# Every second feed-forward weight chunk gets its lower half by an adding transfer instead of a VectorE subtraction

## The chip, the cores and the metric
The kernel runs on one core of a Trainium2 chip. The time is what the device takes for one launch, in microseconds. Before the change three runs took 1796.32 to 1797.32 us, median 1796.88 us. A separate execution was taken by the hardware profiler; durations and waits below come from that one.

## The reference
Two model blocks of two layers each, at 256 positions and width 1024, all in float32. The first block is a mixer of four branches with a context stream. The second block has, in each layer, a sequence mixer (a gated recurrent unit in layer 0, gated linear attention in layer 1) and a convolutional feed-forward part, which is what the change touches:

```python
def causal_dwconv(x, w, b):          # w (K,C), b (C)
    k_width = w.shape[0]
    s = x.shape[1]
    xp = jnp.pad(x, ((0, 0), (k_width - 1, 0), (0, 0)))
    y = b
    for k in range(k_width):
        y = y + xp[:, k:k + s] * w[k]
    return y

def conv_ffn(h, w_up, conv_w, conv_b, w_down):
    u = causal_dwconv(h @ w_up, conv_w, conv_b)
    g, val = jnp.split(u, 2, axis=-1)
    return (jax.nn.gelu(g) * val) @ w_down
# per layer:
#   h = rmsnorm_2(x, norm_g[i, 2]) * (1.0 + sc_f) + sh_f
#   y = conv_ffn(h, ffn_w_up[i], ffn_conv_w[i], ffn_conv_b[i], ffn_w_down[i])
#   x = x + gt_f * rmsnorm_2(y, norm_g[i, 3])
```

w_up is 1024 x 5632 (22 tiles of 128 gate columns and 22 of value columns), w_down 2816 x 1024.

## The kernel before
Activations lie transposed: features on the 128 partitions, the 256 positions along the free dimension. A float32 product is made of three matmuls of a reduced-precision type (float32r): each operand is split into an upper half (the value rounded to that type) and a lower half (the value minus the upper half), and `mm3` adds upper x upper, upper x lower and lower x upper; the lower half of the weight is read by the third of each three.

Weights stream in chunks of 128 x 1024 (512 KB), one for each tile of 128 output columns. `load` brings one: SyncE issues the transfer into a raw tile `wr` (pool `wp`, 3 buffers), ScalarE writes the upper half `wh`, VectorE writes the lower half `wl` as `wr - wh`. `wh` and `wl` have 4 buffers each (`NW = 4`), so four chunks are held: when TensorE has finished with a chunk, `drop` lets the next load begin. `tile_gemm` takes a chunk and does 8 x 3 matmuls of 128 x 256 with it.

`ffn` first does four tiles at once (`start4`), while the normalised input is made, and then loops over the other 20 pairs of gate and value tiles: for each pair two chunks, two accumulators (one from each of two PSUM pools, `pm` and `pa`), the convolution of width 3 (ScalarE takes the last tap and the bias out of PSUM, VectorE adds two taps), GELU on ScalarE, the product on VectorE, and the split of the result (`r`, upper half on ScalarE, lower on VectorE). In the first layer this loop also runs `gla_prepare`, which clears ten buffers of the next layer on ScalarE, one step for each pair. After the loop `project_out` multiplies by w_down, again chunk by chunk.

The order of instructions on each engine is fixed when the program is built: a scheduler places them by its own estimate of when things become ready. On an engine they run strictly in that order, so an instruction that waits holds up all behind it; the same holds for the transfers that SyncE or GpSimd issue. In the first block and the start of the second, SyncE's queue also carries the rows of the modulation matrices (`ad`, two buffers), which VectorE multiplies and sums (`matvec`, `junk`). GpSimd does almost nothing: eight loads of 512 KB (`wf`, line 287) before the second block, and four small operations at the end.

Of the kernel before, what the change touches and what calls it, by code (L numbers as in the profile page):

```python
# [9 lines left out]
F32 = mybir.dt.float32  # L10
# [4 lines left out]
ALU = mybir.AluOpType  # L15
# [70 lines left out]
class Sum:  # L86


    def __init__(self, k=None, *tiles):
        self.k, self.acc, self.last = k, None, None  # L90
        self.tiles = list(tiles)
# [13 lines left out]
class Core:  # L105
    NW = 4

    def __init__(self, nc, tc, ctx, A):
        self.nc, self.tc, self.A = nc, tc, A
        pool = lambda n, b, **k: ctx.enter_context(tc.tile_pool(name=n, bufs=b, **k))  # L110
        self.cst = pool("cst", 1)
        self.wp = pool("wp", 3)
        self.whl = pool("whl", self.NW)
        self.xp = pool("xp", 1)
        self.sml = pool("sml", 16)
        self.rowp = pool("rowp", 2)
        self.mm = pool("mm", 4, space=PSUM)
        self.aux = pool("aux", 4, space=PSUM)
        self.hiq, self.loq = deque(), deque()
        self.src, self.ready, self.held = deque(), deque(), 0  # L120
        self.credit = 0.0
        self.last = self.late = None
        self.wide, self.tiles = 0, 0
        self.uid = 0
        self.pumps, self.spare, self.ratio = -100, 0.0, 0
        self.rows, self.raws = deque(), deque()
        self.marks = deque(maxlen=10)
# [129 lines left out]
    def load(self, src):  # L257
        n = 1
        for d in src.shape[1:]:
            n *= d  # L260
        raw = self.wp.tile([P, 1024], F32, tag="wr", name=self.nm("wr"))
        dst = raw[:, :n]
        if len(src.shape) == 3:
            dst = dst.rearrange("p (a b) -> p a b", a=src.shape[1])
        with self.behind():
            self.lastload = self.nc.sync.dma_start(out=dst, in_=src).ins
        hi = self.whl.tile([P, 1024], F32R, tag="wh", name=self.nm("wh"))
        lo = self.whl.tile([P, 1024], F32R, tag="wl", name=self.nm("wl"))

        def high():  # L270
            self.act(hi[:, :n], raw[:, :n])

        def low():
            self.tt(lo[:, :n], raw[:, :n], hi[:, :n].bitcast(F32), ALU.subtract)
        if self.late is None:
            with self.behind():
                high()
                low()
        else:
            self.late.extend([high, low])  # L280
        return hi, lo
# [1291 lines left out]
    def ffn(self, i, xs, mk, nxt):  # L1573
        w = self.A["ffu"][i]
        for c in range(2, NFF):
            self.src.extend([w[c], w[NFF + c]])
        self.src.extend(self.out_chunks(self.A["ffd"][i], NFF))
        fw = lambda k, c: self.par("ffn_conv_w_2", i * 132 + k * 44 + c)
        acts = []

        def conv(ps, c):
            t = self.T1()
            self.act(t, ps, AF.Identity, scale=fw(2, c), bias=self.par("ffn_conv_b_2", i * 44 + c))
            self.stt(t[:, 1:], ps[:, :S - 1], fw(1, c), t[:, 1:], ALU.mult, ALU.add)
            self.stt(t[:, 2:], ps[:, :S - 2], fw(0, c), t[:, 2:], ALU.mult, ALU.add)
            return t

        def glu(c, pg, pv):
            g = conv(pg, c)
            self.act(g, g, AF.Gelu_apprx_tanh)  # L1590
            v = conv(pv, NFF + c)
            self.tt(g, g, v, ALU.mult)
            acts.append(self.split1(g))

        ps, hs = self.start4(mk, S)
        self.wide = 2
        self.hiq.append(self.squares(xs))
        glu(0, ps[0], ps[2])
        glu(1, ps[1], ps[3])
        prep = self.gla_prepare() if i == 0 else iter(())  # L1600
        for c in range(2, NFF):
            if c > 3:
                next(prep, None)
            pg = self.tile1(hs)
            glu(c, pg, self.tile1(hs))
        self.wide = 0
        return self.project_out(i, 1, xs, acts, NFF, nxt)

    def gla_prepare(self):
# [213 lines left out]
def build(nc, tc, A):  # L1823
    with ExitStack() as ctx:
        k = Core(nc, tc, ctx, A)
        with ExitStack() as c1:
            k.adp = c1.enter_context(tc.tile_pool(name="adp", bufs=2, reuse_waits="tile"))
            k.setup()
            k.t2 = c1.enter_context(tc.tile_pool(name="t2", bufs=58, reuse_waits="tile"))
            fin = k.first_block()  # L1830
        k.t1 = ctx.enter_context(tc.tile_pool(name="t1", bufs=74, reuse_waits="tile"))
        k.g4 = ctx.enter_context(tc.tile_pool(name="g4", bufs=12, reuse_waits="tile"))
        k.second_block(*fin)

# [53 lines left out]
```

## Time and profile before
| | |
|---|---|
| median of three runs | 1796.88 us |
| profiled execution, its own time | 1793.42 us |
| its span | 1791.5 us |
| TensorE busy | 1735.1 us, 97% |
| VectorE busy | 1394.6 us, 78% |
| ScalarE busy | 890.4 us, 50% |
| GpSimd busy | 9.6 us, 1% |
| feed-forward stage of layer 0 | some 1214 to 1425 us |
| feed-forward stage of layer 1 | some 1564 to 1792 us |

In the profile PE is TensorE (PEld its weight loads), DVE VectorE, ACT ScalarE, POOL GpSimd and SP SyncE; L169 is line 169 of the kernel. A tile is named without its number. "wl<-wr,wh" is an instruction that writes a tile wl and reads a wr and a wh. An arrow in brackets names what ended the idle time ahead of an instruction.

### The profile page before, as it was taken

What the parts mean: (1) busy time and instruction counts of PE and PEld (TensorE: products, weight loads), DVE (VectorE), ACT (ScalarE), POOL (GpSimd) and SP (SyncE); (2) the same over time, 40 slices, a digit from 0 to 9 for tenths busy, and PEclk for the clock granted to TensorE, in tenths of its full rate; (3) what the DMA queues carried; (4) which work ended last, traced back from release to release, by engine and by line L of the source; (5) the groups of instructions that cost most, each with busy time, mean ns of one, the idle gap of its engine ahead of it and who ended that gap; (6) DMA issues with size and microseconds to landing.
All of it is one profiled execution on the core that took longest, in us unless ns stands there. A gap on an engine that the chain in (4) does not pass through costs nothing.

```text
span 1791.5 us, 29679 instructions
## 1 busy us (share of the span) xinstructions
PE 1735.1 (97%) x11538; PEld 1556.4 (87%) x11538; DVE 1394.6 (78%) x2564; ACT 890.4 (50%) x1517; POOL 9.6 (1%) x33
## 2 busy tenths in 40 slices
PE   8999999899999898899999999999999999999998
PEld 5777788688878687798999999898999989989998
DVE  4798699974687878899668856778887669788764
ACT  5425432423342233455543555686776565656663
POOL 0000000000000000000000000100000000000000
PEclk9999999999999999999999999999999999999999
DMA  9343244455467877743354335632555633345553
GB/s 345 127 141 117 75 137 136 151 183 175 147 211 266 275 257 267 227 163 130 119 180 150 111 118 188 233 121 95 187 181 177 186 119 105 130 141 189 183 172 117
DMA packets 94300, 301.59 MB, mean 168 GB/s; under 512 B 10048, under 2 KB 11840, under 8 KB 94160
## 3 DMA queue, kind: packets, MB, share of 16 engines
q1 hardware_dynamic: 90528, 292.11, 49.1%
q0 software_dynamic: 1152, 4.19, 0.6%
q10 hardware_dynamic: 2480, 3.39, 0.6%
q8 instruction: 91, 1.49, 0.3%
q14 instruction: 49, 0.40, 0.1%
HBM read 298.61 MB, written 1.05 MB: 167 GB/s over the span
## 4 chain that ended last, share of the span: by engine, by line
PE 71%; DVE 14%; DMA 7%; ACT 4%; issue 4%; SPq 0%; DVEq 0%; ACTq 0%
PE pm L189 55%; PE pa L189 13%; DMA ad<-adaT 6%; DVE t L186 4%; DVE wl L169 3%; ACT t L166 3%; DVE junk L487 2%; DVE t L169 2%; ACT wh L166 1%; PE pa L1113 1%; PE pa L539 1%; PE pa L1705 1%; DVE x L169 0%; ACT r L166 0%; PE pa L591 0%
## 5 line engine op out<-in xcount | busy, mean ns | idle before, releaser
L189 PE MATMUL pm<-r,wh 128*128 128x256 f32 (+2 forms) x5344 | 1216.4, 322 | 28.7 <-ACT r L166 16.7
L189 PEld LDWEIGHTS pm<-r,wh 128*128 128x128 f32 x5344 | 893.3, 191 | 119.3 <-ACT r L166 23.3
L189 PE MATMUL pm<-r,wl 128*128 128x256 f32 (+2 forms) x2672 | 847.8, 319 | 0.5 <-DVE wl L169 0.5
L166 ACT ACTIVATE wh<-wr 128x1024 fp32r<-128x1024 f32 (+1 forms) x408 | 426.1, 1049 | 547.3 <-PE pm L189 398.7
L169 DVE TENSOR_TENSOR wl<-wr,wh 128x1024 fp32r<-128x1024 f32 (+1 forms) x408 | 492.7, 1211 | 199.0 <-ACT wh L166 192.0
L189 PEld LDWEIGHTS pm<-r,wl 128*128 128x128 f32 x2672 | 510.2, 191 | 36.8 <-issue 1.6
L487 DVE SCALAR_TENSOR_TENSOR junk<-ad,sb_c 128x1024 bf16<-128x1024 f32 x128 | 156.5, 1223 | 41.7 <-DMA ad<-adaT 38.5
L189 PE MATMUL pa<-r,wh 128*128 128x256 f32 (+1 forms) x864 | 169.5, 293 | 5.7 <-ACT r L166 5.4
L189 PEld LDWEIGHTS pa<-r,wh 128*128 128x128 f32 x864 | 138.7, 193 | 9.4 <-ACT r L166 5.8
L169 DVE TENSOR_TENSOR t<-t,t 128x256 f32<-128x256 f32 (+2 forms) x278 | 126.4, 471 | 14.2 <-ACT t L166 11.8
L186 DVE SCALAR_TENSOR_TENSOR t<-t,cfw,t 128x482 f32<-128x482 f32 (+29 forms) x240 | 130.3, 602 | 0.0
L189 PE MATMUL pa<-r,wl 128*128 128x256 f32 (+1 forms) x432 | 124.7, 293 | 0.0
L166 ACT ACTIVATE r<-t 128x256 fp32r<-128x256 f32 (+1 forms) x116 | 53.5, 469 | 113.6 <-DVE t L169 82.1
L166 ACT ACTIVATE t<-pm 128x256 f32<-128x256 f32 (+1 forms) x180 | 82.0, 456 | 19.6 <-PE pm L189 19.5
L189 PE MATMUL pa<-t,t 128*64 128x128 f32 (+3 forms) x668 | 88.0, 337 | 0.6 <-ACT t L166 0.3
L189 PEld LDWEIGHTS pa<-r,wl 128*128 128x128 f32 x432 | 83.4, 193 | 1.3
L189 PEld LDWEIGHTS pa<-t,t 128*64 128x64 f32 (+2 forms) x668 | 66.3, 163 | 15.4 <-issue 4.9
L189 PE MATMUL pm<-wh,r 128*128 128x256 f32 x384 | 71.9, 285 | 0.0
L166 ACT ACTIVATE t<-pa 128x512 f32<-128x512 f32 (+2 forms) x102 | 46.0, 512 | 40.9 <-PE pa L189 35.3
L189 PEld LDWEIGHTS pm<-wh,r 128*128 128x128 f32 x384 | 60.5, 191 | 0.5 <-issue 0.4
L186 DVE SCALAR_TENSOR_TENSOR t<-t,pm 128x256 f32<-128x256 f32 (+1 forms) x103 | 56.2, 545 | 6.1 <-PE pm L189 4.7
L169 DVE TENSOR_TENSOR r<-t,r 128x256 fp32r<-128x256 f32 (+1 forms) x108 | 51.0, 479 | 10.5 <-ACT r L166 10.5
(209 smaller groups left out, 1244.6 us busy)
## 6 DMA issues: line engine op xcount, KB each, us to landing
wr<-win SPq DMA_DIRECT2D x172, 512.0 KB, 3.4
ad<-adaT SPq DMA_DIRECT2D x96, 512.0 KB, 4.4
wr<-ffu SPq DMA_DIRECT2D x88, 512.0 KB, 3.3
ad<-wmodT SPq DMA_DIRECT2D x32, 512.0 KB, 3.3
wr<-wbr SPq DMA_DIRECT2D x32, 512.0 KB, 4.2
wr<-ffd SPq DMA_DIRECT2D x32, 512.0 KB, 3.6
wr<-gli SPq DMA_DIRECT2D x24, 512.0 KB, 3.3
t<-wmodN SPq DMA_DIRECT2D x32, 256.0 KB, 5.3
```

Source lines behind the costliest of these rows:

```text
L166: return self.nc.scalar.activation(out=out, in_=in_, func=func, **k)
L169: self.marks.append(self.nc.vector.tensor_tensor(out=out, in0=a, in1=b, op=op).ins)
L186: self.marks.append(self.nc.vector.scalar_tensor_tensor(out=out, in0=a, scalar=s, in1=b, op0=op0, op1=op1).ins)
L189: self.nc.tensor.matmul(out=out, lhsT=lhsT, rhs=rhs, start=start, stop=stop)
L487: self.nc.vector.scalar_tensor_tensor(out=self.junk, in0=raw, scalar=0.5, in1=v, op0=ALU.mult, op1=ALU.mult, accum_out=o)
L539: self.nc.tensor.matmul(out=bank[:, nt * j + t:nt * j + t + 1], lhsT=q[:, t * P:(t + 1) * P], rhs=self.inv[inv], start=first and m == 0 an ...
L1113: nc.tensor.transpose(pt[:, kk * P:(kk + 1) * P], s, self.ident)
L1705: nc.tensor.matmul(out=o, lhsT=cb[:, 7 - jj:7 - jj + P], rhs=b8(hd_(X, h))[:, :, jj:8], start=(jj == 0 and h % 2 == 0), stop=(jj == 7), sk ...
```

## The change
From the first pair of the loop in `ffn` to its end, every second chunk that is loaded gets its lower half in another way: ScalarE writes the negative of the upper half into `wl`, and GpSimd issues a transfer from `wr` to `wl` that adds on arrival (`accum_op`). The value is the same, `wr - wh`. The raw tiles get a fourth buffer, for which two temporaries of the first block (2 KB a partition each) and four of the second (1 KB each) go. Line numbers grow by 1 to 8 in the changed file.

```diff
-        self.wp = pool("wp", 3)
+        self.wp = pool("wp", 4)
...
+        self.loads, self.share = 0, 0
...
+        self.loads += 1
+        summed = self.share and self.loads % self.share == 0
+
         def low():
-            self.tt(lo[:, :n], raw[:, :n], hi[:, :n].bitcast(F32), ALU.subtract)
+            if summed:
+                self.act(lo[:, :n], hi[:, :n].bitcast(F32), scale=-1.0)
+                self.nc.gpsimd.dma_start(out=lo[:, :n].bitcast(F32), in_=raw[:, :n], accum_op=ALU.add)
+            else:
+                self.tt(lo[:, :n], raw[:, :n], hi[:, :n].bitcast(F32), ALU.subtract)
...
-        self.wide = 2
+        self.wide, self.share = 2, 2
...
-        self.wide = 0
+        self.wide = self.share = 0
...
-            k.t2 = c1.enter_context(tc.tile_pool(name="t2", bufs=58, reuse_waits="tile"))
+            k.t2 = c1.enter_context(tc.tile_pool(name="t2", bufs=56, reuse_waits="tile"))
...
-        k.t1 = ctx.enter_context(tc.tile_pool(name="t1", bufs=74, reuse_waits="tile"))
+        k.t1 = ctx.enter_context(tc.tile_pool(name="t1", bufs=70, reuse_waits="tile"))
```

ScalarE in the loop of the layer 1 feed-forward stage, about one pair of chunks, before (`wh` and `wr` belong to weight chunks, `t` and `r` to the results of earlier pairs, `prm` holds the taps):

```order
L166 ACTIVATE wh_16830<-wr_16828 128x1024
L166 ACTIVATE t_16682<-t_16682 128x256
L166 ACTIVATE wh_16875<-wr_16873 128x1024
L166 ACTIVATE r_16692<-t_16682 128x256
L166 ACTIVATE t_16758<-pm_16696,prm 128x256
L166 ACTIVATE t_16763<-pa_16727,prm 128x256
L166 ACTIVATE wh_16906<-wr_16904 128x1024
L166 ACTIVATE t_16758<-t_16758 128x256
```

The same place in the changed kernel:

```order
L167 ACTIVATE wh_16853<-wr_16851 128x1024
L167 ACTIVATE wl_16854<-wh_16853 128x1024
L167 ACTIVATE t_16704<-t_16704 128x256
L167 ACTIVATE wh_16899<-wr_16897 128x1024
L167 ACTIVATE r_16714<-t_16704 128x256
L167 ACTIVATE t_16781<-pm_16718,prm 128x256
L167 ACTIVATE t_16786<-pa_16749,prm 128x256
L167 ACTIVATE wh_16930<-wr_16928 128x1024
L167 ACTIVATE wl_16931<-wh_16930 128x1024
```

The negated copy stands right behind the upper half of the same chunk, ahead of the GELU (`t<-t`).

ScalarE in the loop of layer 0, where `gla_prepare` clears a buffer (`g<-nul`), before:

```order
L166 ACTIVATE wh_13088<-wr_13086 128x1024
L166 ACTIVATE r_12869<-t_12859 128x256
L166 ACTIVATE g_12717<-nul 128x1024
L166 ACTIVATE t_12936<-pm_12874,prm 128x256
L166 ACTIVATE t_12941<-pa_12905,prm 128x256
L166 ACTIVATE wh_13134<-wr_13132 128x1024
L166 ACTIVATE t_12936<-t_12936 128x256
```

The same place in the changed kernel:

```order
L167 ACTIVATE wh_13017<-wr_13015 128x1024
L167 ACTIVATE r_12798<-t_12788 128x256
L167 ACTIVATE g_12721<-nul 128x1024
L167 ACTIVATE t_12866<-pm_12803,prm 128x256
L167 ACTIVATE t_12871<-pa_12834,prm 128x256
L167 ACTIVATE wl_13018<-wh_13017 128x1024
L167 ACTIVATE wh_13066<-wr_13064 128x1024
```

Here the rounding, the clear and two evictions stand between the upper half and the negated copy.

VectorE in the loop of layer 1, about one pair of chunks, before:

```order
L169 TENSOR_TENSOR wl_16831<-wr_16828,wh_16830 128x1024
L169 TENSOR_TENSOR t_16682<-t_16682,t_16687 128x256
L169 TENSOR_TENSOR wl_16876<-wr_16873,wh_16875 128x1024
L169 TENSOR_TENSOR r_16693<-t_16682,r_16692 128x256
L186 SCALAR_TENSOR_TENSOR t_16758<-pm_16696,prm,t_16758 128x255
L186 SCALAR_TENSOR_TENSOR t_16763<-pa_16727,prm,t_16763 128x255
L186 SCALAR_TENSOR_TENSOR t_16758<-pm_16696,prm,t_16758 128x254
L186 SCALAR_TENSOR_TENSOR t_16763<-pa_16727,prm,t_16763 128x254
```

The same place in the changed kernel:

```order
L170 TENSOR_TENSOR t_16704<-t_16704,t_16709 128x256
L170 TENSOR_TENSOR wl_16900<-wr_16897,wh_16899 128x1024
L170 TENSOR_TENSOR r_16715<-t_16704,r_16714 128x256
L187 SCALAR_TENSOR_TENSOR t_16781<-pm_16718,prm,t_16781 128x255
L187 SCALAR_TENSOR_TENSOR t_16786<-pa_16749,prm,t_16786 128x255
L187 SCALAR_TENSOR_TENSOR t_16781<-pm_16718,prm,t_16781 128x254
L187 SCALAR_TENSOR_TENSOR t_16786<-pa_16749,prm,t_16786 128x254
```

One of the two lower halves of a pair is gone; the rest keeps its order.

## Rows read from the trace of the kernel before
**Rows 1.** The page, busy us and share of the span, by engine.
```profile
PE 1735.1 (97%) x11538; PEld 1556.4 (87%) x11538; DVE 1394.6 (78%) x2564; ACT 890.4 (50%) x1517; POOL 9.6 (1%) x33
```
**Rows 2.** Busy time by stretches: length, engines with instruction counts, clock, DMA share, GB/s.
```profile
1250.00:1300.00 50.00, 49.76 (x404) 48.67 (x403) 42.21 (x78) 34.48 (x56) 0.00 (x0) 1.00 0.53 180
1300.00:1350.00 50.00, 50.00 (x419) 50.00 (x418) 40.76 (x69) 38.95 (x62) 0.00 (x0) 1.00 0.55 184
...
1650.00:1700.00 50.00, 50.00 (x419) 50.00 (x418) 39.49 (x69) 32.29 (x53) 0.00 (x0) 1.00 0.54 186
```
**Rows 3.** The chain, layer 1 loop: start, length, what, how many.
```profile
1657.47 2.88 PE pa L189 x24
1660.35 2.88 PE pm L189 x24
```
**Rows 4.** Waits from 1600 to 1715 us: total, times, longest.
```profile
ACT wh L166 <- PE pm L189: 23.8, 17, 1.4
...
PEld pm L189 <- ACT wh L166: 0.2, 1, 0.2
```
**Rows 5.** Groups by line, 1225 to 1355 us: busy us, mean ns, idle before.
```profile
L169 DVE TENSOR_TENSOR wl<-wr,wh 128x1024 fp32r<-128x1024 f32 x40 | 48.7, 1220 | 12.0 <-ACT wh L166 12.0
...
L166 ACT ACTIVATE wh<-wr 128x1024 fp32r<-128x1024 f32 x40 | 42.0, 1055 | 20.5 <-PE pa L189 14.1 <-PE pm L189 5.7 <-DMA wr<-ffu 0.2
```
**Rows 6.** Instructions in order of time, layer 1 loop: start, length, what.
```profile
1642.90 0.40 PE L189 MATMUL pm<-r,wh 128*128 128x256 f32 x2
...
1642.98 1.06 ACT L166 ACTIVATE wh<-wr 128x1024 fp32r<-128x1024 f32 x1 [0.61 <-PE pa L189]
1644.02 0.42 ACT L166 ACTIVATE t<-t 128x256 f32<-128x256 f32 x1
```
**Rows 7.** ScalarE in order of time, layer 0 loop with a clear.
```profile
1307.68 1.06 ACT L166 ACTIVATE wh<-wr 128x1024 fp32r<-128x1024 f32 x1 [0.70 <-PE pa L189]
1308.64 0.40 ACT L166 ACTIVATE r<-t 128x256 fp32r<-128x256 f32 x1
1308.95 1.04 ACT L166 ACTIVATE g<-nul 128x1024 f32<-128x1024 f32 x1
1309.90 0.54 ACT L166 ACTIVATE t<-pm,prm 128x256 f32<-128x256 f32 x1
1310.35 0.55 ACT L166 ACTIVATE t<-pa,prm 128x256 f32<-128x256 f32 x1
1310.80 1.05 ACT L166 ACTIVATE wh<-wr 128x1024 fp32r<-128x1024 f32 x1
```
**Rows 8.** Tile wf, the GpSimd load at 1154.6 us: issue ns, landing.
```profile
L287 POOL DMA_DIRECT2D wf<-rgw x1: 528/528/528, 1154.6 to 1154.6; - x1
...
DMA to landing us min/median/max: 4.7/4.7/4.7
```
**Rows 9.** Tile wf, the GpSimd load at 1144.9 us.
```profile
L287 POOL DMA_DIRECT2D wf<-rgw x1: 713/713/713, 1144.9 to 1144.9; - x1
...
DMA to landing us min/median/max: 6.3/6.3/6.3
```
**Rows 10.** Transfers by line: count, size, median us to landing.
```profile
wr<-ffu SPq DMA_DIRECT2D x88, 512.0 KB, 3.3
```
**Rows 11.** Tile wf, all eight GpSimd loads: count, issue ns, first and last start.
```profile
L287 POOL DMA_DIRECT2D wf<-rgw x4: 528/537/713, 1144.9 to 1155.1; - x4
L287 POOL DMA_DIRECT2D wf<-rgo x4: 707/716/728, 1155.6 to 1157.7; - x4
...
DMA to landing us min/median/max: 4.7/6.8/10.6
```
**Rows 12.** Busy time by stretches in the first block.
```profile
610.00:620.00 10.00, 7.17 (x31) 5.34 (x29) 9.72 (x16) 3.00 (x5) 0.00 (x0) 0.96 0.79 267
620.00:630.00 10.00, 6.36 (x15) 4.21 (x16) 8.65 (x14) 2.24 (x4) 0.00 (x0) 0.53 0.85 277
...
690.00:700.00 10.00, 5.42 (x14) 4.02 (x13) 8.60 (x14) 2.90 (x6) 0.00 (x0) 0.71 0.86 291
```

## The prediction
> **What bounds the kernel now.** I read the page's busy line first, then the busy time by stretches of the two feed-forward stages, then the chain and the waits inside them, then single instructions. The busy line puts TensorE at 97% and VectorE at 78% [rows 1]; that is an average over stages. In the feed-forward stages the picture is sharper: from 1300 to 1350 us and from 1650 to 1700 us TensorE is busy for all 50 us at the full granted clock, while VectorE is at 40 of 50 and ScalarE at 39 and 32 of 50 [rows 2]. The chain there is TensorE alone, one weight chunk after another, 2.88 us each, alternating between the two PSUM pools [rows 3]; that is 24 matmuls at 0.12 us. Nobody waits for VectorE's lower halves: ScalarE's upper half waits for TensorE to give a weight buffer back, and TensorE's whole wait for weights from 1600 to 1715 us is 0.2 us [rows 4]. So the work that is taken off VectorE is hidden work, and what decides is whether the new way of making a lower half is in time.
>
> **What is removed.** 40 subtractions (20 in each feed-forward stage, counted in the changed order), 1.22 us each [rows 5], 49 us of VectorE. Beside a TensorE without gaps this is worth nothing. Only where a stage starts is there a gap to win: the 50 us from 1250 hold 404 matmuls, the next 50 hold 419 [rows 2], 15 x 0.12 = 1.8 us, so at most 3.6 us for two stages. Few summed chunks are prepared that early, so I take 1.5.
>
> **What is added on ScalarE.** 40 negated copies. I price them like the copy of the same shape, 1.05 us [rows 5]: 42 us. From 1300 to 1350 that is nearly 9 more on 39 of 50 [rows 2], still under 50; hidden, but the copy stands in line, and the adding transfer starts only behind it.
>
> **What is added as a wait.** A weight buffer is used by every fourth chunk. A chunk's upper half can start when the chunk four before it ends, and its lower half is first read by the third matmul of its own turn: 3 x 2.88 + 0.24 = 8.88 us later. Into this must fit the upper half, the copy, the issue and the landing of the transfer. Before, the same stretch held upper half and subtraction, 1.06 + 1.23 us plus queueing, with some 5 us to spare.
> What ScalarE does ahead of the transfer follows from the order and the rows:
> - Second stage: the next chunk begins at 1642.90 and the upper half starts at 1642.98 [rows 6]; the copy follows directly, so it ends some 2.15 us after the chunk's end. Left for the transfer: 8.88 - 2.15 = 6.7 us, for 20 chunks.
> - First stage, while ScalarE also clears buffers for the next layer: upper half, rounding, clear, two evictions and only then the copy. In the rows the place of the copy comes at 1310.80, 3.1 us after the upper half's start [rows 7]; it ends at 4.2 to 4.3. Left: 4.6 us, for 6 chunks. Two with short clears keep 5.3. In two chunks the upper half of the next chunk (which waits another 2.88 us for TensorE) and a GELU stand ahead of the copy: 2.96 + 1.04 + 0.42 + 1.06 = 5.5 us, left 3.4. The other ten keep about 6.4.
>
> **The price of the adding transfer.** No row shows one. The nearest is a plain 512 KB load issued by GpSimd: with nothing of that queue ahead of it 4.7 us [rows 8] and 6.3 us [rows 9] from issue to landing. The ends: below, SyncE's load of that size, 3.3 us [rows 10]; above, the last of six GpSimd loads in a row, 10.6 us [rows 11]. The addition also has to read its target. From 1300 to 1350 a DMA share of 0.55 moved 184 GB/s [rows 2], that is 9.2 MB or 17.5 loads in 27.5 us of all engines: 1.57 us a load. I add one such read to the mean of 4.7 and 6.3: D = 5.5 + 1.57 = 7.0 us.
> The Trainium skill (Collectives: The Full Stack, The bandwidth ceiling: the fold count and why AG ≠ RS ≠ AR) says that a reducing transfer runs at half the rate of a copy because both sources are read through one ring. No run here shows it yet; it asks for the same second read, and with the slower row, 6.3 + 1.57 = 7.9, it would make the loss worked out below some 38 us instead of 19.5.
>
> **The sum.** Summed chunks are every second one, so each reuses the buffer of the second summed chunk before it. An overrun delays TensorE once for each pair of them, not for each. With D = 7.0: second stage 10 x (7.0 - 6.7) = 2.5 to 3 us. First stage: two of the 3.4 kind, which share a buffer line, 2 x 3.6 = 7.2; three pairs of the 4.6 kind, 3 x 2.4 = 7.2; the plain ones, 3 x 0.6 behind them and about 0.8 ahead. That is 17, together 19.5. The same sum gives 3 at D = 4.7, 9 at 6.0, 50 at 8.5, 80 at 10. A second reckoning agrees: two loads and one addition with two reads hold the engines for 2 x 1.57 + 3.14 = 6.3 us for each two chunks, which TensorE does in 5.76; over 40 pairs that is 21 us. At one read's cost it is 4.7 us and the engines are no bound.
> **What moves elsewhere.** The fourth raw buffer lets SyncE issue weight loads about one chunk earlier in the whole program. The only stretch where loads reach the end is the first block, where modulation rows feed VectorE; TensorE idles there 11 us in three slices of 10 [rows 12]. Those rows have two buffers of their own, and between the same two matvecs the queue holds as many loads as before, so I take 0 (ends: -11, and +2 for a load that goes ahead of a row). The smaller pools of temporaries (58 to 56, 74 to 70) leave the order of TensorE's matmuls the same but for a few neighbours; I take 0.
> Sum: +19.5 - 1.5 = +18 us. The profiled execution took 1793.42 us, its span 1791.5; the median of the runs is 3.5 us above it. So 1811.4 in the profile's terms, 1815 as a median.
>
> **Rivals.**
> 1. The transfer is hidden (no change). The addition costs no more than the faster plain load, D up to about 5; the loss is 0 to 4 us, against which stand up to 3.6 of gaps. Time 1796 to 1800. For it: slack of 6.7 us in most chunks. Against: 4.7 us was a load that reads once. The Trainium skill (DMA: Bandwidth & Descriptors, Anatomy of one DMA — SWDGE (gpsimd) path) fits such a transfer as 2.0 us plus its bytes at 436 GB/s, an estimate of 3.2 us here, and by that nothing would stall. The two rows above measured 4.7 and 6.3 for that size on that queue and disagree. Chance 0.16.
> 2. Faster. The deeper ring of raw buffers brings the modulation rows earlier and closes the idle slices of the first block; the place is 610 to 630 and 690 to 700 us, the price up to 11 us, and with the 3.6 us at the stages' starts at most 15. It decides if the transfer stays under 4.6 us or if D is 6 and the 11 come whole. Time 1782 to 1793. Against: the weight loads in that stretch are followed by the same rows in the same order. Chance 0.12.
> 3. Much slower. The additions use the engines for more than two reads, or queue behind each other and the raw loads, D = 10: +80, 1877 us. Or the stalls cost clock: after TensorE had idled 2.8 us between 610 and 620 and on into the next slice, the granted clock from 620 to 630 was 0.53, about the lower level of 1.2 GHz [rows 12]; ten microseconds at half rate lose some 5, and a dozen such stalls 60. Chance 0.12.
> That the 40 halves are not moved at all is no rival: the order shows them.
>
> **How the numbers follow.** Forecast (D from 5.5 to 9, +6 to +60 less up to 3.6) 0.60; rivals 0.16, 0.12 and 0.12. What a measurement can tell from no change is about 0.2%, 3.6 us. Faster: 0.12. Within: 0.13 of the first rival and 0.02 of the forecast's low end, 0.15. Slower: 0.73. The range 1793 to 1862 reaches from the edge of the second rival to D about 9.4 (+65), and leaves out most of rivals 2 and 3; the forecast's own range is 1801 to 1856.
>
> **What the new profile would show.** Right: in the feed-forward stages TensorE waits for weights with the adding transfer as releaser, first in the stretch with the clears, gaps of 2 to 4 us, few gaps in the second stage; from issue to landing 6 to 8 us; VectorE 49 us less, ScalarE 42 more; both stages end some 20 us later in total, all else within 3 us. Wrong, if TensorE stays without gaps in the stages (rival 1), if the second stage loses as much as the first (D above 8, rival 3), or if the time moves before 1200 us (rival 2).

## The result, and the profile after

The changed kernel took 1834.72 us (median of four runs, 1832.24 to 1837.34); the kernel before took 1796.6 us on the same chip. The ratio is 1.0217, 95% interval 1.0203 to 1.0232: slower by 38 us. The forecast was 1815, so the direction is right and the loss is twice the one forecast.

The profiled execution took 1834.25 us, 40.8 more than the one of before. To see where, each stage is measured in the matmuls' start times of the trace, between pauses of TensorE that every kernel here makes at the same places of the program (1.0 us ahead of the first feed-forward stage, 2.2 us behind it, 2.0 to 2.2 us ahead of the second, 0.7 us behind that). The stage of layer 0 so measured is the loop, the projection behind it and the start of the next layer (1248 to 1487 us before). "Pauses" is taken over all matmuls of the stage that start more than 0.25 us after the one before; it is the sum of what their distance has over the usual 0.12 us:

| | before | after | difference |
|---|---|---|---|
| up to the first stage | 1248.4 us | 1249.7 us | +1.3 |
| stage of layer 0 (its pauses) | 238.3 (3.6) | 265.7 (24.3) | +27.4 (+20.6) |
| between the stages | | | +0.4 |
| stage of layer 1 (its pauses) | 205.4 (4.7) | 216.0 (13.3) | +10.6 (+8.7) |
| from there to the end of the span | 9.0 us | 10.2 us | +1.2 |

So 38.0 of the 41 us lie in the two stages, 29.3 of them as pauses. The rest, 8.7, is nearly all clock, as later rows show.

The busy line of the page answers to [rows 1]. VectorE has lost 41 us and 40 instructions (the subtractions of this shape by themselves fell by the 49 of the forecast, from 492.7 to 444.0), ScalarE has gained 34 and 40, TensorE's busy time has grown by 14 with the same number of matmuls:

```profile
PE 1748.9 (95%) x11538; PEld 1566.9 (86%) x11538; DVE 1353.4 (74%) x2524; ACT 924.8 (50%) x1557; POOL 44.0 (2%) x73
```

The busy times by stretches answer to [rows 2], with the same columns. TensorE now has gaps of some 4 to 6 us in each of them, and in the last the DMA engines are at 0.94 of their time where they were at 0.54:

```profile
1250.00:1300.00 50.00, 44.58 (x354) 43.09 (x355) 35.68 (x70) 35.49 (x56) 3.60 (x5) 1.00 0.66 188
1300.00:1350.00 50.00, 44.50 (x336) 43.32 (x336) 23.58 (x46) 36.06 (x54) 5.90 (x7) 0.93 0.85 221
1650.00:1700.00 50.00, 46.41 (x379) 45.39 (x378) 29.43 (x57) 36.81 (x57) 6.85 (x8) 1.00 0.94 256
```

The view of the line that issues the adding transfers has no row before; [rows 8, 9 and 11] were its nearest. It shows the 40 transfers, who waited for them (us, times), and the time from issue to landing:

```profile
L280 POOL DMA_DIRECT2D wl<-wr x40: 847/856/925, 1271.1 to 1756.8; - x40
...
  PEld pa L190: 22.6, 18
...
  PEld pm L190: 4.9, 3
...
DMA to landing us min/median/max: 4.4/6.0/8.7
```

TensorE's weight loads wait 22.6 + 4.9 = 27.5 us for them, in 21 waits, nearly the whole 29.3 of added pauses. In [rows 4], over 115 us of the layer 1 stage, the whole wait for weights was 0.2. The median of 6.0 us is less than the 7.0 of the forecast, and still the loss is twice as large.

The loads of the weights have become slower too; this list of transfers answers to [rows 10], where the median was 3.3 us:

```profile
wr<-ffu SPq DMA_DIRECT2D x88, 512.0 KB, 4.4
wl<-wr POOLq DMA_DIRECT2D x40, 512.0 KB, 6.0
```

One stall of the layer 0 stage in order of time (start, length, engine, line, what, idle time ahead and its releaser) shows how the loss is made; [rows 6 and 7] show the same instructions undisturbed:

```profile
1277.04 0.88 POOL L280 DMA_DIRECT2D wl<-wr  x1 [4.97 <-ACT wl L167]
...
1284.73 0.19 PEld L190 LDWEIGHTS pa<-r,wl 128*128 128x128 f32 x1 [1.55 <-DMA wl<-wr]
1284.74 1.58 SPq L267 DMA_DIRECT2D wr<-ffu  x2
...
1290.22 1.06 ACT L167 ACTIVATE wh<-wr 128x1024 fp32r<-128x1024 f32 x1 [4.82 <-DMA wr<-ffu]
1291.31 1.06 ACT L167 ACTIVATE wl<-wh 128x1024 fp32r<-128x1024 f32 x1
...
1292.66 0.86 POOL L280 DMA_DIRECT2D wl<-wr  x1 [8.28 <-ACT wl L167]
...
1299.48 0.19 PEld L190 LDWEIGHTS pa<-r,wl 128*128 128x128 f32 x1 [3.18 <-DMA wl<-wr]
```

The transfer issued at 1277.04 lands 7.6 us later, at about 1284.7. Two things go on within 0.1 us of that: TensorE, which had waited 1.55 us for this lower half, and SyncE, which issues a load of raw weights at 1284.74. That load had no buffer, since the transfer reads the raw tile until it lands. It lands late, so ScalarE stands 4.82 us before the upper half at 1290.22, the copy and the next transfer come behind it, and TensorE waits 3.18 us at 1299.48. One late transfer is paid twice: at once, and again some chunks on.

The clock, in slices of 10 us. The third value from the right is the granted clock:

```profile
1310.00:1320.00 10.00, 10.00 (x86) 10.00 (x84) 4.27 (x9) 8.67 (x13) 0.86 (x1) 1.00 0.86 247
1320.00:1330.00 10.00, 7.20 (x48) 7.00 (x47) 3.56 (x7) 5.12 (x8) 0.86 (x1) 0.83 0.93 254
...
1760.00:1770.00 10.00, 8.03 (x55) 7.82 (x54) 4.76 (x11) 5.83 (x11) 0.00 (x0) 0.83 0.73 220
```

Five such slices of the two loops stand at 0.83 or 0.84, so part of each ran at the lower of the two levels (1.2 GHz, not 2.4): 10 x 0.17 = 1.7 us each, 8.5 in all. In that from 1320, TensorE had just waited 3.00 us (up to 1323.05), in that from 1760, 2.2 us.

### The profile page after: what moved, and what is told of

The parts are those of the page before. It is cut to its first block, busy times and chain, and to the rows that moved or that the text cites. A ratio compares the mean times of both kernels' runs of the same rounds, so it can differ in the third digit from the quotient of the medians.

```text
span 1832.5 us, 29732 instructions
## 1 busy us (share of the span) xinstructions
PE 1748.9 (95%) x11538; PEld 1566.9 (86%) x11538; DVE 1353.4 (74%) x2524; ACT 924.8 (50%) x1557; POOL 44.0 (2%) x73
## 4 chain that ended last, share of the span: by engine, by line
PE 67%; DMA 12%; DVE 11%; ACT 6%; issue 4%; DVEq 0%; ACTq 0%; POOLq 0%; SPq 0%
PE pm L190 53%; PE pa L190 11%; DMA ad<-adaT 6%; DMA wl<-wr 5%; ACT t L167 3%; DVE junk L495 3%; DVE wl L170 2%; DVE t L187 2%; ACT wh L167 2%; DVE t L170 2%; PE pa L1121 1%; DMA wr<-ffu 1%; ACT wl L167 1%; PE pa L547 1%; PE pa L1713 1%
## 5 line engine op out<-in xcount | busy, mean ns | idle before, releaser
L170 DVE TENSOR_TENSOR wl<-wr,wh 128x1024 fp32r<-128x1024 f32 x368 | 444.0, 1210 | 198.1 <-ACT wh L167 191.2
L190 PE MATMUL pa<-r,wh 128*128 128x256 f32 (+1 forms) x864 | 174.2, 298 | 5.7 <-ACT r L167 5.4
L190 PE MATMUL pa<-r,wl 128*128 128x256 f32 (+1 forms) x432 | 128.7, 302 | 19.0 <-DMA wl<-wr 18.9
L190 PEld LDWEIGHTS pa<-r,wl 128*128 128x128 f32 x432 | 85.3, 197 | 24.1 <-DMA wl<-wr 22.6
```

The source lines that it names most:

```text
L170: self.marks.append(self.nc.vector.tensor_tensor(out=out, in0=a, in1=b, op=op).ins)
L190: self.nc.tensor.matmul(out=out, lhsT=lhsT, rhs=rhs, start=start, stop=stop)
```

## The experiments

Two theories at first. **L**, the forecast's own: each adding transfer lands later than TensorE wants it, by its own duration against its own slack. **C**: two weight loads and an addition take more of the DMA engines' time than TensorE takes for two chunks, and everything that is loaded gets late. A third, **H**, came up on the way and is told where it does. The diffs are against the changed kernel unless they say otherwise; the losses of the stages come from each kernel's profile, measured as in the table above.

**1. The pools alone.**

```diff
-        self.wide, self.share = 2, 2
+        self.wide, self.share = 2, 0
```

> Only the pools of the change (four raw weight buffers instead of three, 70 and 56 temporaries instead of 74 and 58); no chunk is summed. Theory L (the adding transfer of a chunk lands after TensorE wants its lower half, and some of these stalls also cost granted clock): nothing of the 38 us comes from the pools, 1794 to 1800 us. Rival P (the smaller pools of temporaries or the deeper raw ring carry part of the loss): 1805 us or more. A gain below 1793 would show that the deeper ring does help and that the transfers cost more than 38.

Measured: 1794.63 us, ratio 0.9992 (0.9981 to 1.0004). The deeper ring of raw buffers and the smaller pools do nothing, as forecast.

**2. Copy and transfer beside the work, onto a tile that nobody reads.**

```diff
-                self.act(lo[:, :n], hi[:, :n].bitcast(F32), scale=-1.0)
-                self.nc.gpsimd.dma_start(out=lo[:, :n].bitcast(F32), in_=raw[:, :n], accum_op=ALU.add)
+                self.tt(lo[:, :n], raw[:, :n], hi[:, :n].bitcast(F32), ALU.subtract)
+                scr = self.G4()
+                self.act(scr[:, :n], hi[:, :n].bitcast(F32), scale=-1.0)
+                self.nc.gpsimd.dma_start(out=scr[:, :n], in_=raw[:, :n], accum_op=ALU.add)
```

> VectorE makes all lower halves as before; the negated copy and the adding transfer of every second chunk still run, but onto a scratch tile that nobody reads, so ScalarE, the DMA engines and the raw buffers carry the change's whole load and only TensorE's wait is gone. Theory L (lateness of what TensorE reads): 1797 to 1805 us, no gap over 1 us in the layer-1 stage, at most two or three in layer 0 where a raw buffer is given back late. Rival C (the 16 DMA engines at 0.94 to 0.95 of their time, or ScalarE, are the bound and every raw load comes late): 1820 us or more, with TensorE waiting for VectorE's halves or ScalarE for raw loads.

Measured: 1829.39 us, ratio 1.0204 (1.0169 to 1.0239). L by itself falls here: no lower half waits for a transfer, and nearly the whole loss is still there, 28.2 us in layer 0 and 6.9 in layer 1. What ScalarE waits for in the layer 0 stage (total us, times, longest) says where it comes from; before, it waited 0.2 us for them in [rows 5]:

```profile
ACT wh L167 <- DMA wr<-ffu: 29.2, 14, 6.3
```

**3. The transfer copies instead of adding.**

```diff
-                self.nc.gpsimd.dma_start(out=lo[:, :n].bitcast(F32), in_=raw[:, :n], accum_op=ALU.add)
+                self.nc.gpsimd.dma_start(out=lo[:, :n].bitcast(F32), in_=raw[:, :n])
```

> The transfer copies instead of adding (the addition is left out: the lower halves hold the raw weights). It gives the price of the addition. Theory L with the addition as a second read: from issue to landing falls from 6.0 us by about 1.3 to 1.6 us, the engines hold a transfer for 1.6 us instead of 2.8, and the loss falls from 38 to 5 to 12 us: 1802 to 1809 us. If adding costs nothing beside a copy, the time stays at 1832 to 1837 and so does the 6.0 us.

Measured: 1805.13 us, ratio 1.0051 (1.0036 to 1.0066). This is the price of the addition. The queue's share of all 16 engines from 1270 to 1410 us, in this kernel and in the changed one (name, packets, MB, share):

```profile
q0 software_dynamic: 2880, 10.49, 19.6%
```

```profile
q0 software_dynamic: 2837, 10.38, 41.1%
```

Over 140 us and 20 transfers (19.8 by the bytes of the second) a copy holds the engines for 1.37 us, an addition for 2.9 us, 2.1 times as long; from issue to landing they take 4.2 and 6.0 us in the median. The forecast's second read (1.57 x 2 = 3.14 us) was near. The Trainium skill (Collectives: The Full Stack, The bandwidth ceiling: the fold count and why AG ≠ RS ≠ AR) gives 1.93 for the reducing step of a collective against its copying step, from the two source reads; this trace, of another kind of transfer, agrees within a tenth. These are sums of the packets' times, and packets can overlap: in experiment 13 the share of 16 engines passes 1.00. They are no hard limit of what the engines can do.

**4. The lower half last.** The 8 matmuls with the lower half of a weight chunk run behind the 16 with the upper half.

```diff
+        if self.share:
+            for k in range(n):
+                sl = slice(w0 + k * step, w0 + k * step + P)
+                self.mmul(out, W[0][:, sl], xs[k][0], k == 0, False)
+                self.mmul(out, W[0][:, sl], xs[k][1], False, False)
+            for k in range(n):
+                sl = slice(w0 + k * step, w0 + k * step + P)
+                self.mmul(out, W[1][:, sl], xs[k][0], False, k == n - 1)
+            return
```

> In the feed-forward chunks the 16 matmuls with the upper half of the weights run first and the 8 with the lower half last; nothing else moves. The lower half is wanted after 16 matmuls instead of 2: 14 x 0.12 = 1.7 us more slack. Theory L: the layer-1 stage (overruns of 0.7 to 2.1 us) loses its gaps almost wholly, layer 0 (1 to 3 us) keeps some 5 us and no clock is lost: 1800 to 1808 us. Rival C (the DMA engines are full, what is late stays late by more and more): 1825 us or more, since a rate is not helped by slack.

Measured: 1830.99 us, ratio 1.0199 (1.0183 to 1.0214). L's number is missed by 23 us; 1.7 us more room for every chunk gave 4, or 3 against the kernel before on the same chip, which is not clear of the noise.

After these four C stood alone, and the next four went on from it. **R** in them is the theory that the raw buffer held by the transfer is the cause.

**5. As 2, but the transfer reads the upper half** (diff against the kernel of experiment 2)**.**

```diff
-                self.nc.gpsimd.dma_start(out=scr[:, :n], in_=raw[:, :n], accum_op=ALU.add)
+                self.nc.gpsimd.dma_start(out=scr[:, :n], in_=hi[:, :n].bitcast(F32), accum_op=ALU.add)
```

> As the experiment with the transfers onto an unread scratch tile (VectorE makes all lower halves), but the adding transfer reads the upper half instead of the raw weights, so that it holds no raw buffer either: what is left of the change is 40 copies on ScalarE and 40 adding transfers on the DMA engines. Theory C (the engines' time: two loads of 1.6 us and an addition of 2.9 us make 6.1 us for each two chunks, which TensorE does in 5.76): raw loads still land late, 1815 us or more, layer 1 alone still loses 5 to 12 us. Theory R (the transfer gives its raw buffer back 5 to 8 us late, and the next raw load starts late by that): back to 1796 to 1802 us.

Measured: 1821.1 us, ratio 1.0151 (1.0133 to 1.0169), which looks like C. The stages say otherwise: layer 1 loses nothing (-0.7 us) with the DMA share at 1.00 to 1.03, and layer 0 loses 24.7. The wait there shows what the expectation overlooked: the transfer now holds the weight buffer `wh`.

```profile
ACT wh L167 <- DMA g<-wh: 21.9, 10, 3.4
```

**6. Every fourth chunk summed.**

```diff
-        self.wide, self.share = 2, 2
+        self.wide, self.share = 2, 4
```

> Every fourth chunk is summed by a transfer instead of every second, 20 in all. Theory C (engine time): 4 x 1.6 + 2.9 = 9.3 us for four chunks against 11.52 us of TensorE, so the engines have room and the loss goes almost wholly, 1796 to 1803 us. Theory L (each transfer is late by itself, 6 us against its slack): half of the stalls stay, 1810 to 1818 us.

Measured: 1798.34 us, ratio 1.0025 (1.0012 to 1.0039): half of the transfers cost a tenth of the loss. The loss isn't a sum over transfers.

**7. A fifth raw buffer** (and 66 and 54 temporaries instead of 70 and 56)**.**

```diff
-        self.wp = pool("wp", 4)
+        self.wp = pool("wp", 5)
```

> The change with five raw weight buffers instead of four (66 and 56 temporaries). Theory C (engine time): a deeper ring doesn't add engine time, 1825 to 1836 us. Theory R (raw buffers held by the transfers): the raw loads start a chunk earlier, 1797 to 1812 us, and the gain lies mostly in layer 0.

Measured: 1831.14 us, ratio 1.0203 (1.0184 to 1.0222). R alone falls too; the gain is not clear of the noise.

**8. The next layer's buffers cleared by VectorE.**

```diff
+        def clear(t, v=0.0):
+            self.nc.vector.memset(t, v)
...
-                pin(self.fill(t, self.nul))
+                clear(t)
```

> The change with the buffers that are cleared for the next layer during the layer-0 feed-forward stage cleared by VectorE instead of ScalarE, so that the negated copy stands up to 1.1 us earlier in ScalarE's line. Theory L: the layer-0 loop loses some 15 us instead of 27, 1818 to 1825 us. Theory C: 1830 us or more, layer 0 as before.

Measured: 1823.44 us, ratio 1.0160 (1.0135 to 1.0185), the stage of layer 0 13.4 us longer than before instead of 27.4, that of layer 1 8.8 instead of 10.6 (in the profile of the fastest run, 5.7 us under the median). ScalarE's line makes most of what layer 0 loses more than layer 1; this part of L holds.

Now the waits of 4 and 7 were laid beside each other, in the layer 0 stage. With the lower half last (experiment 4), TensorE waits little for the transfers, ScalarE waits for raw weights and TensorE for ScalarE:

```profile
ACT wh L167 <- DMA wr<-ffu: 23.4, 9, 4.6
...
PEld pm L190 <- ACT wh L167: 8.0, 5, 3.6
...
PEld pa L190 <- DMA wl<-wr: 6.4, 3, 2.5
```

With a fifth raw buffer (experiment 7) the wait for raw weights is gone, and TensorE waits for the transfers:

```profile
PEld pa L190 <- DMA wl<-wr: 13.7, 10, 3.9
...
ACT wh L167 <- DMA wr<-ffu: 0.9, 1, 0.9
```

That is theory H: full engines make the transfers late, and a late transfer does its harm through what hangs on it, the raw buffer and TensorE's wait, either of which is enough. The buffer alone is experiment 2 (33 us lost), the wait nearly alone experiment 7 (36).

**9. The copies alone**, experiment 2 without the transfer (diff against its kernel).

```diff
-                self.nc.gpsimd.dma_start(out=scr[:, :n], in_=raw[:, :n], accum_op=ALU.add)
```

> VectorE makes all lower halves; of the change only the 40 negated copies on ScalarE are left, onto an unread scratch tile, and no adding transfer. From 1310 to 1350 us that puts some 7 copies of 1.05 us on ScalarE's 31 of 40. Theory C (the engines' time is the main cause, ScalarE's line only lengthens it): 1794 to 1800 us. Rival A (moving the clears gave 13 of 38 us back, so ScalarE by itself is a bound in layer 0): 1806 us or more, all of it in layer 0.

Measured: 1799.51 us, ratio 1.0020 (1.0010 to 1.0029), 3.6 us; in its profile the stage of layer 0 is 4.0 us longer and that of layer 1 0.6. ScalarE by itself is no bound, but at 37 of 40 us it leaves TensorE a few gaps:

```profile
1310.00:1350.00 40.00, 38.78 (x312) 37.53 (x311) 30.51 (x53) 37.03 (x55) 0.00 (x0) 1.00 0.50 168
```

**10. Transfers that hold nothing** (diff against the kernel of experiment 2): they read a tile that is cleared once.

```diff
-                self.nc.gpsimd.dma_start(out=scr[:, :n], in_=raw[:, :n], accum_op=ALU.add)
+                self.nc.gpsimd.dma_start(out=scr[:, :n], in_=self.still[:, :n], accum_op=ALU.add)
...
+        k.still = k.g4.tile([P, 1024], F32, tag="still", name="still", bufs=1)
+        nc.vector.memset(k.still, 0.0)
```

> As the run before with the 40 adding transfers put back, but reading a tile that never changes: they hold neither a raw buffer nor a weight buffer, and TensorE waits for none of them. They only use the DMA engines (66 temporaries make room for the tile). Theory C in its strict form (full engines delay the raw loads, and that alone costs the time): 1808 us or more. Theory H (full engines are harmless as long as nothing waits for, or is held by, the transfer that is late; the loss comes from TensorE's wait and from what the transfer holds): 1795 to 1803 us, though the DMA share of the stages is about 1.0.

Measured: 1805.92 us, ratio 1.0053 (1.0035 to 1.0071), between the two expectations, 2.9 us above H's range and 2.1 below C's. Layer 1 goes by H, and the 8.9 us that layer 0 still loses are more than H had. In layer 1 TensorE has no gap (the stage is 0.7 us shorter than before) though the DMA share is 1.02, transfers land after 8.1 us and raw loads after 6.9:

```profile
1640.00:1680.00 40.00, 40.00 (x335) 40.00 (x335) 33.08 (x57) 32.71 (x50) 5.99 (x7) 1.00 1.02 288
1680.00:1720.00 40.00, 40.00 (x336) 40.00 (x335) 32.45 (x57) 32.55 (x50) 5.99 (x7) 1.00 1.02 275
```

```profile
wr<-ffu SPq DMA_DIRECT2D x25, 512.0 KB, 6.9
g<-still POOLq DMA_DIRECT2D x17, 512.0 KB, 8.1
```

This and experiment 2 differ in the tile that the transfer reads (and in the four temporaries that make room for it). The raw buffer that it holds is worth 1829.4 - 1805.9 = 23 us. Full engines by themselves, over the copies of experiment 9, are worth some 6, all in layer 0.

**11. Half of each lower half by a transfer.**

```diff
-                self.act(lo[:, :n], hi[:, :n].bitcast(F32), scale=-1.0)
-                self.nc.gpsimd.dma_start(out=lo[:, :n].bitcast(F32), in_=raw[:, :n], accum_op=ALU.add)
+                m = n // 2
+                self.act(lo[:, :m], hi[:, :m].bitcast(F32), scale=-1.0)
+                self.nc.gpsimd.dma_start(out=lo[:, :m].bitcast(F32), in_=raw[:, :m], accum_op=ALU.add)
+                self.tt(lo[:, m:n], raw[:, m:n], hi[:, m:n].bitcast(F32), ALU.subtract)
```

> Still 40 summed chunks, but only the left 512 columns of each lower half by negated copy and adding transfer, the right ones by VectorE. Two loads of 1.6 us and an addition of some 1.45 us hold the engines for 4.65 us of TensorE's 5.76. Theory C: the loss goes almost wholly, 1796 to 1804 us, and from issue to landing falls to 4 to 5 us. Rival W (40 waits for a transfer behind ScalarE's line, whatever its size): 1812 us or more.

Measured: 1805.84 us (1798.28 to 1808.5), ratio 1.0063 (1.0043 to 1.0084); the median is 1.8 us above C's range and far under W's. The same 40 transfers, with half of the engines' time in them, cost less than a third; from issue to landing they took 3.9 us in the median, a little under the 4 to 5 expected.

**12 and 13. Both walls moved; then a fifth pair of weight buffers as well.** Experiment 4's order of the matmuls in both; the diff is against that kernel, its last two lines are in 13 alone. The temporaries shrink by as much as the buffers take.

```diff
-        self.wp = pool("wp", 4)
+        self.wp = pool("wp", 5)
...
-    NW = 4
+    NW = 5
```

> The change with two of its walls moved at once, each of which gave little alone: five raw buffers (66 and 54 temporaries) and the 8 matmuls with the lower half behind the 16 with the upper half. Theory H (a late transfer does its harm through the two things that hang on it, the raw buffer that it holds and TensorE's wait, and either one suffices): together they give most of the loss back, 1806 to 1818 us, layer 1 within 4 us of before. Theory C (the engines' rate: what is late stays late by more): 1826 us or more.

> As the run before, with a fifth pair of weight buffers as well (58 and 50 temporaries), 2.88 us more room for every chunk. Theory H: what is left is ScalarE's copies (4 us) and the engines' own contention (some 6 us, as in the run whose transfers held nothing), 1799 to 1808 us. Theory C: 1822 us or more.

Measured: 1812.83 us (1803.48 to 1816.25), ratio 1.0108 (1.0083 to 1.0133), and 1802.93 us, ratio 1.0045 (1.0030 to 1.0060). Against the kernel before on the same chip the losses are 35.1 us with the lower half last (experiment 4), 36.4 with the fifth raw buffer (experiment 7), 17.7 with both and 7.8 with the fifth pair of weight buffers as well. So each step alone gave 2 to 3 us, which is not clear of the noise, both together give 20, and 30 of the 38 are back in the end, with all 40 transfers still there and the engines as full:

```profile
1640.00:1680.00 40.00, 40.00 (x335) 40.00 (x335) 24.84 (x49) 32.39 (x50) 5.99 (x7) 1.00 1.04 302
1680.00:1720.00 40.00, 40.00 (x336) 40.00 (x335) 24.85 (x49) 32.55 (x50) 5.99 (x7) 1.00 1.01 272
```

Both times lie in H's ranges; its word on layer 1 in experiment 12, within 4 us of before, is missed (4.8 in the profile of the fastest run). H is borne out in the main; C in its strict form, that the engines' rate itself is the loss, is not: the engines can carry two loads and an addition for each pair of chunks if what is late has room. No version was faster than the kernel before, and TensorE without gaps leaves nothing in these stages that one could win.

## Why the prediction came out as it did

**Right.** The subtractions were worth nothing: VectorE was hidden. The pools were worth nothing (experiment 1). TensorE waits with the adding transfer as releaser, in 21 waits, for 40 transfers, more in layer 0 (27.4 us) than in layer 1 (10.6), and there mostly because the clears stand ahead of the copy (experiment 8). All else moved by 3 us in sum, as forecast. The engines' price of an addition, two reads, was 2.9 us against 3.14.

**Wrong: the term "What is added as a wait", 19.5 us, came out at 38.** Its working took the transfer as a duration, D, against a slack counted from the chunk's end, with everything ahead of the copy as in the rows of before. D was even set too high, 7.0 against a median of 6.0; the forecast's own table gives 9 us for 6.0. That its other estimate, D = 7.9, gives the 38 that were measured is luck. What failed is the premise that ScalarE's upper half starts when TensorE gives the weight buffer back, as in [rows 6]. That needs the raw weights to be there. The raw buffers were set down under "What moves elsewhere", for the first block, with a price of 0; that the adding transfer is a new reader, which holds a raw buffer until it lands, was not counted at all. Ahead of its loads SyncE now waits for the transfers, 20 times in the stage of layer 0 (total us, times, longest), where before it waited there almost only for instructions of VectorE:

```profile
SPq L267 <- DMA wl<-wr: 90.2, 20, 8.0
```

This is what holds back the load of 1284.74 and makes ScalarE wait 4.82 us. Copies and transfers with that buffer in their hands, and without any wait of TensorE's for them, cost 33 us (experiment 2), 23 of them by the buffer (against experiment 10).

How much of the 38 this is in the changed kernel itself can be read chunk by chunk. Of the 27.5 us that TensorE's weight loads wait for the transfers, some 13 (7 waits) stand behind upper halves that started 0.8 to 4 us after the chunk four before had ended, and some 15 (14 waits) behind ones that started within 0.1 us of that. The second part is what the term reckoned, and 19.5 was not too little for it, though its split was off: 9 in layer 0 against 17, 6 in layer 1 against 2.5 to 3. The first part, and the clock's 8.5, are what it had not counted.

**The second reckoning** (6.3 us of the engines for each 5.76 of TensorE, 21 us) was read as a confirmation of the first sum. It is another mechanism. The engines were as full as it says, 0.89 to 0.98 in layer 1 by stretches of 40 us, but full engines alone cost about 6 us (experiment 10); they matter because they stretch the raw loads from 3.3 to 4.4 us (at most from 4.8 to 8.5) and the transfers from a median of 4.5, with half as many of them (experiment 6), to 6.0, with 4.4 and 8.7 as the ends. The sum with one D for all has no place for that spread, though TensorE waits for the late ones and gets nothing back from the early ones.

**The copies** were costed at nothing, hidden in ScalarE's idle time. Alone they cost 3.6 us (experiment 9): at 37 of 40 us busy the cover is too thin.

**The clock** stood in the third rival at 5 us for each stall and was left out of the sum. It fell for 5 of the stalls, at 1.7 us each, 8.5 us; neither nothing nor 60.

**The rivals.** The hidden transfer is out; even a plain copy (experiment 3) lost 9 us, against its 0 to 4. The Trainium skill's fit behind it (DMA: Bandwidth & Descriptors, Anatomy of one DMA — SWDGE (gpsimd) path), an estimate of 3.2 us, compares with a median of 4.2 us for that plain copy in a busy stretch; 6.0 us for an addition is beyond it. The second rival's idle slices in the first block did not close: with the pools alone the ratio is 0.9992. Of the third rival, transfers and raw loads did get in each other's way, but its D of 10 us did not come: no transfer of the changed kernel took over 8.7 us.

## What to carry to other kernels

When work goes from an idle engine to a transfer, list what the transfer reads and writes, and ask for each buffer when it now comes free: a longer reader in a ring of buffers delays the next load as surely as a late result delays its consumer. Where two such walls stand close behind each other, moving one shows next to nothing (2 to 3 us here, within the noise) and both together 20, so a failed remedy doesn't clear its cause. And count the engines' time for each round of the loop: near 100% a transfer's duration is no longer one number, and the late ones set the pace.

## What was not expected of the hardware

- By the times of its packets, from 1270 to 1410 us, a transfer that adds from one tile in SBUF to another takes all 16 engines for 2.9 us for 512 KB, a plain one 1.37 us (experiment 3).
- With the engines at 1.00 to 1.04 of their time TensorE can still run without a gap (experiments 5, 10 and 13), with raw loads landing after 6.5 to 6.9 us instead of 3.3 (experiments 5 and 10).
- Open: the last 1.2 us. From the end of the second stage to the end of the span it takes 1.2 us longer in every kernel with 40 transfers, also at half their size (experiment 11), and not in those with 20 or none. The runs of experiments 8, 11 and 12 spread over 8 to 13 us, and their profiles are of the fastest run, so that the stages of their profiles show less than their medians.
